# Half units of a logsumexp: three TensorE-biased heads, one exponential over two PSUM banks, GpSimd folding

## The chip, the cores and the metric

The kernel runs on 1 core of one Trainium2 chip. The metric is the time of one execution on the device, in microseconds (us). A run is called slow when it is over 1.5% above the fastest run of the same kernel in the same measurement, else fast. Ratios below use fast runs only.

Names: PE is TensorE, PEld its weight loads, ACT is ScalarE, DVE is VectorE, POOL is GpSimd. The clock that a profile shows is the share of PE's full clock that was granted. A warming matmul is one whose result nobody uses; it is there to keep PE busy. "The lock" is the prediction's name for something it assumed: that weighted sums of VectorE with two SBUF inputs and GpSimd's adds hold each other up. The trace of the kernel before had not shown it; the runs below measure it (such a sum 648 ns in "steady", and 416 with its factor in PSUM in "psum7"; GpSimd's third add 492 ns in "rows128" and 386 in "psum7"). A "half unit" is half of a tile of the input: 128 rows of 2048 numbers (1 MB).

## The reference

```python
B, S, D, H = 8, 2048, 2048, 8          # x: (B, S, D) float32, bias: (H, D // H)
x_heads = x.reshape(B, S, H, Dh).transpose(0, 2, 1, 3) + bias[None, :, None, :]
x_tiled = np.repeat(x_heads, 2, axis=2)
mx = x_tiled.max(axis=-1, keepdims=True)
lse = mx.squeeze(-1) + np.log(np.exp(x_tiled - mx).sum(axis=-1))
```

Each row of x holds 8 heads of 256 numbers. For each row and head the kernel needs the logarithm of the sum of exp(x + bias). The 134 MB of x are read once. The kernel subtracts no maximum, and is correct on this draw.

## The kernel before

There are 64 tiles of 2 x 128 rows (2 MB). A head's bias can enter in two ways. PE adds it: a bias matmul and an identity matmul accumulate x + bias in PSUM, and ACT takes the exponential from there. Or ACT takes exp(x), and VectorE multiplies by exp(bias) while it sums (a "weighted sum"). A few heads are added up by GpSimd: it halves the 256 elements by adding halves until 32 are left ("fold"), and VectorE reduces those. The closing stage (tiles 57 to 63) loads and works in half units:

```python
PROMPT_F1 = dict(pe=2, acc=2, g0=8, late=False, fold=1)   # 2 heads biased on PE and summed by ACT, 1 folded
PROMPT_F2 = dict(pe=2, acc=2, g0=8, late=False, fold=2)
SINGLE_F1 = dict(pe=1, acc=1, g0=8, late=False, fold=1)
TRIPLE = dict(pe=3, acc=3, g0=8, late=False, fold=0)
FOLD = 32
STAGES = [
    (0, (BULK,)),
    (54, (MIXED,)),
    (57, (PROMPT_F1, PROMPT_F1)),
    (62, (SINGLE_F1, SINGLE_F1)),
    (63, (PROMPT_F2, TRIPLE)),
]
# ... (cut)
    def put_bias(m, k0, k1):
        # ... (cut: bulk)
        for k in range(k0, k1, rows):
            for c in range(0, n, MM):                 # MM = 512
                # ... (cut)
                mm = nc.tensor.matmul(p, lhsT=ones3, rhs=each_row(b3, c, w, rows),
                                      start=True, stop=False)   # bf16, 3 rows: bias in three parts
    def keep_warm():
        for _ in range(NWARM):
            nc.tensor.matmul(tp[:, 0], lhsT=ident, rhs=ident, start=True, stop=True)

    def sum_biased(t, k, h, bank, p, mm, sums):       # one head: exp and sum by ACT
        act = nc.scalar.activation(out=xts[t % NBUF][:, k, h * Dh : (h + 1) * Dh], in_=p,
                                   func=ACT.Exp, accum_out=sums[:, k, h : h + 1])

    def weigh(t, v, h, dst, after):                   # one head: weighted sum by VectorE
        c = h * Dh
        if c < W0:
            w = one_ps[:, c - V0 : c - V0 + Dh]       # factors in PSUM
        elif c < W2:
            w = w_ps[:, c - W0 : c - W0 + Dh]         # factors in PSUM
        else:
            w = w_sb[:, c - W1 : c - W1 + Dh]         # head 7: factors in SBUF
        # ... (cut: tensor_tensor_reduce, multiply and add)

    def fold(t, k, h0, h1, sums, after):              # multiply by w_sb, then halve to FOLD
        # ... (cut)
```

In a half unit of tiles 57 to 61, before the change, ACT takes one exponential of six heads and two of one head with a sum; VectorE makes five weighted sums; GpSimd multiplies one head by its factors and folds it.

The softmax here doesn't subtract the row's maximum and nothing guards it: scores larger than these inputs give would overflow.

Of the kernel before, what the change touches and what calls it, by code (L numbers as in the profile page):

```python
# [11 lines left out]
ACT = mybir.ActivationFunctionType  # L12
ALU = mybir.AluOpType
# [7 lines left out]
NBUF = 8  # L21

NEARLY = 5

NWARM = 3



# [1 line left out]



BULK = dict(pe=3, acc=1, g0=4, late=True, fold=0)
MIXED = dict(pe=1, acc=1, g0=4, late=False, fold=0)
PROMPT_F1 = dict(pe=2, acc=2, g0=8, late=False, fold=1)
PROMPT_F2 = dict(pe=2, acc=2, g0=8, late=False, fold=2)
SINGLE_F1 = dict(pe=1, acc=1, g0=8, late=False, fold=1)
TRIPLE = dict(pe=3, acc=3, g0=8, late=False, fold=0)
FOLD = 32

STAGES = [
    (0, (BULK,)),
    (54, (MIXED,)),
    (57, (PROMPT_F1, PROMPT_F1)),
    (62, (SINGLE_F1, SINGLE_F1)),
    (63, (PROMPT_F2, TRIPLE)),
]

LAST_COLS = [
    [(0, 512), (1280, 2048), (512, 1280)],  # L50
    [(0, 512), (768, 1280), (1280, 1792), (512, 768), (1792, 2048)],
]

# [2 lines left out]
def kernel(  # L56
# [6 lines left out]
    nc = tc.nc  # L63
    P = nc.NUM_PARTITIONS
    B, S, D = x.shape
    H, Dh = bias.shape
# [4 lines left out]
    T = B * NBLK  # L71
    T_PROMPT = STAGES[1][0]
    T_FACTORS = T // 2
    CPE = BULK["pe"] * Dh
    MM = 512
# [11 lines left out]
    w_sb = sb.tile([P, D - W1], F32, name="w_sb")  # L87
# [153 lines left out]
    n_ps = [0]  # L241


    bank_users = [[], []]

    def on_bank(i, ins):
        for j, u in bank_users[i // 2]:
            if j != i and u.ins.engine != ins.ins.engine:
                tc.declare_no_dep(ins.ins, u.ins, reason="another bank")
        bank_users[i // 2].append((i, ins))  # L250
        return ins

    def put_bias(m, k0, k1):



        if m["late"]:
            pair = pairs[n_ps[0] % 2]
            n_ps[0] += 1
            got = [one_ps, pair[:, 0:MM], pair[:, MM : 2 * MM]]  # L260

            parts = [(ones3, b3)]
            if n_ps[0] <= NEARLY:
                parts = [(ones3[0:1], bparts[:, i]) for i in range(3)]
            for h, p in enumerate(got):
                for i, (lhsT, b) in enumerate(parts):
                    nc.tensor.matmul(  # L267
                        p,
                        lhsT=lhsT,
                        rhs=each_row(b, h * Dh, Dh, K),  # L270
                        start=i == 0,
                        stop=False,
                    )
            return got + [pair]
        n = m["pe"] * Dh
        rows = min(k1 - k0, max(MM // n, 1))
        got = []
        for k in range(k0, k1, rows):
            for c in range(0, n, MM):
                w = min(n - c, MM)  # L280
                bank = n_ps[0] % len(ps)
                p = ps[bank][:, 0 : rows * w]
                n_ps[0] += 1
                mm = nc.tensor.matmul(
                    p,
                    lhsT=ones3,
                    rhs=each_row(b3, c, w, rows),
                    start=True,
                    stop=False,
                )  # L290
                on_bank(bank, mm)
                got.append((k, k + rows, c, w, bank, p))
        return got

    def add_x(m, t, k0, c0, c1, got):


        heads = []
        for ka, kb, c, w, bank, p in got:
            if not c0 <= c < c1:  # L300
                continue
            mm = nc.tensor.matmul(  # L302
                p,
                lhsT=ident,
                rhs=xts[t % NBUF][:, ka:kb, c : c + w],
                start=False,
                stop=True,
            )
            on_bank(bank, on_x(t, mm, [loads[t, k0, c0]]))
            for i in range(0, (kb - ka) * w, Dh):  # L310
                k, cw = divmod(i, w)
                heads.append((ka + k, (c + cw) // Dh, bank, p[:, i : i + Dh], mm))
        return heads

    def keep_warm():
        for _ in range(NWARM):
# [109 lines left out]
        )  # L426
        last_uses[t].append(on_x(t, ttr, [after]))

    def fold(t, k, h0, h1, sums, after):


        v = xts[t % NBUF][:, k, h0 * Dh : h1 * Dh]
        done = nc.gpsimd.tensor_tensor(  # L433
            out=v, in0=v, in1=w_sb[:, h0 * Dh - W1 : h1 * Dh - W1], op=ALU.mult
        )
        on_x(t, done, [after])
        v = v.rearrange("p (h j) -> p h j", j=Dh)
        n = Dh
        while n > FOLD:
            n //= 2  # L440
            done = nc.gpsimd.tensor_tensor(  # L441
                out=v[:, :, 0:n], in0=v[:, :, 0:n], in1=v[:, :, n : 2 * n], op=ALU.add
            )
            on_x(t, done, [])

        def add_up():
            red = nc.vector.tensor_reduce(
                out=sums[:, k, h0:h1],
                in_=v[:, :, 0:FOLD],
                op=ALU.add,  # L450
                axis=mybir.AxisListType.X,
            )
            on_x(t, red, [done])

        return add_up
# [60 lines left out]
    def flush(later_work):  # L516
        for f in later_work:
            f()
        later_work.clear()

    for t in range(T):
# [4 lines left out]
        for k0, k1, c0, c1 in pieces(t):  # L526
# [5 lines left out]
            if m["late"]:  # L532
                pe_part = late_heads(m, t, bias_here, sums)
            else:
                heads = add_x(m, t, k0, c0, c1, bias_here)

                def pe_part(t=t, heads=heads, sums=sums):
                    for k, h, bank, p, mm in heads:
                        sum_biased(t, k, h, bank, p, mm, sums)

            if c0 == 0:
                if next_units and not m["late"]:
                    bias_there = put_bias(*next_units.pop(0))
                if t > T_PROMPT and m["g0"] == H:
                    keep_warm()
                if m["g0"] < H:
                    add = g_add(m, t, k0, k1)
                if t < T - 1 or k0 == 0:
                    flush(for_pool)
# [1 line left out]
                first_factors()  # L551
            h0 = max(c0 // Dh, m["pe"])
            h1 = min(c1 // Dh, m["g0"])
            hf = max(h0, min(h1, H - m["fold"]))
            if h0 < h1 and not m["late"]:
                done = exp_inplace(
                    t, xt[:, k0:k1, h0 * Dh : h1 * Dh], loads[t, k0, c0]
                )
                if hf < h1:
                    for_pool.append(fold(t, k0, hf, h1, sums, done))  # L560
            if c0 == 0:
                flush(for_pe)
            if not m["late"]:
                for k in range(k0, k1):
                    for h in range(h0, hf):
                        weigh(
                            t,
                            xt[:, k, h * Dh : (h + 1) * Dh],
                            h,
                            sums[:, k, h : h + 1],  # L570
                            done,
                        )
# [55 lines left out]
```

## Time and profile before

| | before |
|---|---|
| time, first measurement | 325.62 us median of 3 (325.56 to 325.81) |
| span of the profile | 323.1 us |
| time less span of the profiled run | 325.31 - 323.1 = 2.2 us |
| data read, rate | 134.23 MB, 419 GB/s |
| last row of the sums done on VectorE | 319.64 us |

In a page row of groups, the columns are: line, engine, operation, output and inputs with shapes, count, busy us and mean ns of one, then the idle time just before such instructions and what ended it. In a row of the timeline: start, length, instruction, and in brackets the idle time before it. Two such rows of VectorE in the kernel before, which the prediction did not show, matter for what follows:

```profile
305.38 0.19 DVE L447 TENSOR_REDUCE R_last<-xb 128x1 f32<-128x32 f32 x1 [0.15 <-POOL xb L441]
307.46 0.18 DVE L447 TENSOR_REDUCE R_last<-xb 128x1 f32<-128x32 f32 x1 [0.20 <-POOL xb L441]
```

Once per half unit, from 305 us, VectorE waits 0.15 to 0.20 us for a fold. It has worked off its backlog and has some slack, though not much: under a tenth of the 2.08 us that a half unit takes.

### The profile page before, as it was taken

Reading aid. Unit: us, or ns where it says so; the run is one execution under the profiler, and the core shown is the slowest. Engines: PE = TensorE matmul, PEld = TensorE weight load, DVE = VectorE, ACT = ScalarE, POOL = GpSimd, SP = SyncE. Lnnn points to the kernel's source line nnn. Section 1 sums busy time; section 2 is a strip of 40 time slices with the busy share of each in tenths; the row PEclk is TensorE's granted clock in tenths of the full one; section 3 lists DMA queues with packets and bytes.
Section 4 is the critical chain, followed back from the end, with each engine's and each line's share of the span. In section 5 each row is a group of like instructions: output and inputs, shape, how many; then the busy total and the mean of one; then the engine's idle time right before and its main releaser. Section 6 shows DMA issues by size and latency. Waiting matters only on the chain.

```text
span 323.1 us, 2398 instructions
## 1 busy us (share of the span) xinstructions
PE 270.3 (84%) x691; PEld 102.9 (32%) x691; DVE 283.9 (88%) x306; ACT 265.8 (82%) x426; POOL 287.7 (89%) x120
## 2 busy tenths in 40 slices
PE   5999999889978769977869886888997786599984
PEld 2333333333323223322323322333333232035442
DVE  1037779999999998999899899898999999999995
ACT  1148679889869976988888978889998998899995
POOL 6939998999999999999999999999999999858874
PEclk9979799979979996998997997997999999559998
DMA  8999999999999999999999999999999999999995
GB/s 311 457 402 454 450 400 439 450 402 446 438 414 446 432 418 443 430 422 447 422 426 441 422 434 442 404 426 430 432 422 431 430 428 425 416 422 421 419 401 170
DMA packets 8830, 135.42 MB, mean 419 GB/s; under 512 B 1041, under 2 KB 1425, under 8 KB 2417
## 3 DMA queue, kind: packets, MB, share of 16 engines
q1 hardware_dynamic: 8720, 135.27, 98.6%
q8 instruction: 5, 0.08, 0.1%
q14 instruction: 7, 0.06, 0.0%
q10 hardware_dynamic: 98, 0.01, 0.0%
HBM read 134.23 MB, written 1.05 MB: 419 GB/s over the span
## 4 chain that ended last, share of the span: by engine, by line
DMA 40%; POOL 18%; ACT 17%; PE 14%; DVE 9%; issue 0%; SPq 0%; DVEq 0%
DMA xb<-in_x_dram 40%; POOL xb L376 18%; ACT xb L382 11%; DVE R L401 6%; PE pair L326 5%; PE one_ps L326 3%; PE pair L267 3%; ACT xb L357 2%; PE one_ps L267 2%; DVE xb L417 2%; PE pair L219 1%; ACT xb L337 1%; DVE xb L394 1%; ACT res L471 1%; ACT xb L344 1%; DMA brow<-in_bias_dram 1%
## 5 line engine op out<-in xcount | busy, mean ns | idle before, releaser
L376 POOL TENSOR_TENSOR xb<-xb,b_rep 128x2048 f32<-128x2048 f32 x57 | 257.6, 4539 | 20.7 <-DMA xb<-in_x_dram 20.6
L401 DVE TENSOR_REDUCE R<-xb 128x14 f32<-128x3584 f32 (+1 forms) x56 | 214.5, 3830 | 1.9
L382 ACT ACTIVATE xb<-xb 128x2560 f32<-128x2560 f32 (+5 forms) x77 | 157.1, 2050 | 10.3 <-POOL xb L376 10.1
L326 PE MATMUL pair<-xb,ident 128*128 128x512 f32 x216 | 114.3, 656 | 0.0
L326 PE MATMUL one_ps<-xb,ident 128*128 128x512 f32 x108 | 67.5, 710 | 11.5 <-DMA xb<-in_x_dram 11.5
L344 ACT ACTIVATE xb<-pair 128x1024 f32<-128x1024 f32 x54 | 55.5, 1027 | 23.2 <-PE pair L326 23.0
L326 PEld LDWEIGHTS pair<-xb,ident 128*128 128x128 f32 x216 | 46.2, 214 | 61.3 <-issue 61.3
L394 DVE TENSOR_TENSOR xb<-xb,w_ps 128x512 f32<-128x512 f32 x54 | 36.7, 681 | 26.2 <-ACT xb L382 26.2
L337 ACT ACTIVATE xb<-one_ps 128x256 f32<-128x256 f32 x108 | 40.0, 380 | 6.6 <-PE one_ps L326 6.6
L267 PEld LDWEIGHTS <-ones 3*128 3x128 bf16 (+1 forms) x192 | 16.9, 95 | 80.8 <-issue 71.4
L267 PE MATMUL one_ps<-b,ones 3*128 3x512 bf16 x49 | 18.6, 380 | 25.4 <-ACT xb L337 25.3
L267 PE MATMUL pair<-b,ones 3*128 3x512 bf16 x98 | 29.0, 375 | 0.0
L326 PEld LDWEIGHTS one_ps<-xb,ident 128*128 128x128 f32 x108 | 17.2, 200 | 33.9 <-DMA xb<-in_x_dram 18.0
L302 PE MATMUL pair<-xb,ident 128*128 128x512 f32 (+1 forms) x36 | 21.7, 689 | 5.7 <-DMA xb<-in_x_dram 5.7
L417 DVE CUSTOM_DVE_ANT_0 xb<-xb,w_ps 128x256 f32<-128x256 f32 x61 | 22.4, 418 | 0.0
L337 ACT ACTIVATION_READ_ACCUMULATOR xb<-one_ps 128x1 f32 x108 | 22.3, 207 | 0.0
L441 POOL TENSOR_TENSOR xb<-xb 128x128 f32<-128x128 f32 (+3 forms) x39 | 13.8, 355 | 3.1
L433 POOL TENSOR_TENSOR xb<-xb,w_sb 128x256 f32<-128x256 f32 (+1 forms) x13 | 10.0, 771 | 5.2 <-ACT xb L382 4.5
L317 PE MATMUL tp<-ident 128*128 128x128 f32 x84 | 13.7, 302 | 0.0
L317 PEld LDWEIGHTS tp<-ident 128*128 128x128 f32 x84 | 11.1, 200 | 3.5 <-issue 3.0
L357 ACT ACTIVATE xb<-pair 128x256 f32<-128x256 f32 x33 | 11.9, 364 | 0.0
L417 DVE CUSTOM_DVE_ANT_0 xb<-xb,one_ps 128x256 f32<-128x256 f32 x27 | 10.6, 415 | 0.1
(42 smaller groups left out, 83.4 us busy)
## 6 DMA issues: line engine op xcount, KB each, us to landing
xb<-in_x_dram SPq DMA_DIRECT2D x20, 4096.0 KB, 21.5
xb<-in_x_dram SPq DMA_DIRECT2D x17, 2048.0 KB, 22.7
xb<-in_x_dram SPq DMA_DIRECT2D x12, 1024.0 KB, 22.7
xb<-in_x_dram SPq DMA_DIRECT2D x4, 256.0 KB, 13.2
out_dram<-res SPq DMA_DIRECT2D x1, 896.0 KB, 6.7
xb<-in_x_dram SPq DMA_DIRECT2D x2, 384.0 KB, 15.8
xb<-in_x_dram SPq DMA_DIRECT2D x2, 128.0 KB, 6.3
out_dram<-res_last SPq DMA_DIRECT2D x1, 128.0 KB, 1.7
```

The lines of the kernel that those rows point to most:

```text
L267: nc.tensor.matmul(p, lhsT=lhsT, rhs=each_row(b, h * Dh, Dh, K), start=i == 0, stop=False,)
L302: mm = nc.tensor.matmul(p, lhsT=ident, rhs=xts[t % NBUF][:, ka:kb, c : c + w], start=False, stop=True,)
L317: nc.tensor.matmul(tp[:, 0], lhsT=ident, rhs=ident, start=True, stop=True)
L326: mm = nc.tensor.matmul(p, lhsT=ident, rhs=xts[t % NBUF][:, :, h * Dh : (h + 1) * Dh], start=False, stop=True,)
L337: act = nc.scalar.activation(out=xts[t % NBUF][:, k, 0:Dh], in_=got[0][:, k * Dh : (k + 1) * Dh], func=ACT.Exp, accum_out=sums[:, k, 0:1],)
L344: act = nc.scalar.activation(out=xts[t % NBUF][:, :, Dh : m["pe"] * Dh].rearrange("p k (h j) -> p h k j", j=Dh), in_=got[-1].rearrange("p ...
L357: act = nc.scalar.activation(out=xts[t % NBUF][:, k, h * Dh : (h + 1) * Dh], in_=p, func=ACT.Exp, accum_out=sums[:, k, h : h + 1],)
L376: add = nc.gpsimd.tensor_tensor(out=v, in0=v, in1=each_row(b_rep, c - G0, D - c, k1 - k0), op=ALU.add)
L382: return on_x(t, nc.scalar.activation(out=v, in_=v, func=ACT.Exp), [after])
L394: mul = nc.vector.tensor_tensor(out=f, in0=f, in1=each_row(w_ps, m["pe"] * Dh - W0, n, k1 - k0), op=ALU.mult,)
L401: red = nc.vector.tensor_reduce(out=sums[:, k0:k1, h0:H], in_=v.rearrange("p k (h j) -> p k h j", j=Dh), op=ALU.add, axis=mybir.AxisListTy ...
L417: ttr = nc.vector.tensor_tensor_reduce(out=v, in0=v, in1=w, scale=1.0, scalar=0.0, op0=ALU.mult, op1=ALU.add, accum_out=dst,)
```

## The change

The intent: relieve ACT, which paces the closing stage. Three heads are biased on PE; ACT takes their exponential in one instruction over two PSUM banks, without sums; GpSimd folds all three, and has no multiply any more, because the bias is already in. One mode serves all half units from tile 57 on, but the last. The core of the diff:

```diff
-NWARM = 3
+NWARM = 8
-PROMPT_F1 = dict(pe=2, acc=2, g0=8, late=False, fold=1)
-PROMPT_F2 = dict(pe=2, acc=2, g0=8, late=False, fold=2)
-SINGLE_F1 = dict(pe=1, acc=1, g0=8, late=False, fold=1)
+FOLDED = dict(pe=3, acc=0, g0=8, late=False)
-    (57, (PROMPT_F1, PROMPT_F1)),
-    (62, (SINGLE_F1, SINGLE_F1)),
-    (63, (PROMPT_F2, TRIPLE)),
+    (57, (FOLDED, FOLDED)),
+    (63, (FOLDED, TRIPLE)),
@@
+    def exp_biased(t, k, n, heads):
+        _, _, bank, _, mm = heads[-1]
+        act = nc.scalar.activation(
+            out=xts[t % NBUF][:, k, 0 : n * Dh],
+            in_=pairs[bank // 2][:, 0 : n * Dh],
+            func=ACT.Exp,
+        )
+        on_bank(bank, on_x(t, act, [mm]), both=True)
+        return act
@@ fold
-        done = nc.gpsimd.tensor_tensor(
-            out=v, in0=v, in1=w_sb[:, h0 * Dh - W1 : h1 * Dh - W1], op=ALU.mult
-        )
+        v = xts[t % NBUF][:, k, 0 : n * Dh].rearrange("p (h j) -> p h j", j=Dh)
+        w = Dh
+        done = after
+        while w > FOLD:
+            w //= 2
+            add = nc.gpsimd.tensor_tensor(
+                out=v[:, :, 0:w], in0=v[:, :, 0:w], in1=v[:, :, w : 2 * w], op=ALU.add
+            )
+            done = on_x(t, add, [done])
@@ main loop
+                    if m["acc"] == 0:
+                        done = exp_biased(t, k, m["pe"], heads)
+                        for_pool.append(fold(t, k, m["pe"], sums, done))
+                        return
@@
-                if next_units and not m["late"]:
-                    bias_there = put_bias(*next_units.pop(0))
-                if t > T_PROMPT and m["g0"] == H:
+                if t > T_PROMPT and m["g0"] < H:
                     keep_warm()
@@
-            if c0 == 0:
+            if c0 == 0 or t == T - 1 and k0 == 0:
                 flush(for_pe)
+            if c0 == 0 and next_units and not m["late"]:
+                bias_there = put_bias(*next_units.pop(0))
 (cut: bank tracking, the last tile's columns, removal of the arguments h0, h1)
```

The warming matmuls move too: three per half unit before, none in the half units after; eight at each of tiles 55 and 56 instead.

More of the change, by code (lines that the diff above doesn't have):

```diff
@@ L23 @@
 NEARLY = 5
-NWARM = 3
-BULK = dict(pe=3, acc=1, g0=4, late=True, fold=0)
-MIXED = dict(pe=1, acc=1, g0=4, late=False, fold=0)
-PROMPT_F1 = dict(pe=2, acc=2, g0=8, late=False, fold=1)
-PROMPT_F2 = dict(pe=2, acc=2, g0=8, late=False, fold=2)
-SINGLE_F1 = dict(pe=1, acc=1, g0=8, late=False, fold=1)
-TRIPLE = dict(pe=3, acc=3, g0=8, late=False, fold=0)
+NWARM = 8
+BULK = dict(pe=3, acc=1, g0=4, late=True)
+MIXED = dict(pe=1, acc=1, g0=4, late=False)
+FOLDED = dict(pe=3, acc=0, g0=8, late=False)
+TRIPLE = dict(pe=3, acc=3, g0=8, late=False)
 FOLD = 32
@@ L43 @@
     (54, (MIXED,)),
-    (57, (PROMPT_F1, PROMPT_F1)),
-    (62, (SINGLE_F1, SINGLE_F1)),
-    (63, (PROMPT_F2, TRIPLE)),
+    (57, (FOLDED, FOLDED)),
+    (63, (FOLDED, TRIPLE)),
 ]
 LAST_COLS = [
-    [(0, 512), (1280, 2048), (512, 1280)],
+    [(0, 768), (1280, 2048), (768, 1280)],
     [(0, 512), (768, 1280), (1280, 1792), (512, 768), (1792, 2048)],
@@ L244, with on_bank @@
     bank_users = [[], []]
-    def on_bank(i, ins):
-        for j, u in bank_users[i // 2]:
-            if j != i and u.ins.engine != ins.ins.engine:
+    def on_bank(i, ins, both=False):
+        pair = i // 2
+        i = None if both else i
+        for j, u in bank_users[pair]:
+            if None not in (i, j) and j != i and u.ins.engine != ins.ins.engine:
                 tc.declare_no_dep(ins.ins, u.ins, reason="another bank")
-        bank_users[i // 2].append((i, ins))
+        bank_users[pair].append((i, ins))
         return ins
@@ L275, in put_bias @@
         n = m["pe"] * Dh
+        if n > MM:
+            n_ps[0] += n_ps[0] % 2
         rows = min(k1 - k0, max(MM // n, 1))
@@ L427, in weigh, with fold @@
         last_uses[t].append(on_x(t, ttr, [after]))
-    def fold(t, k, h0, h1, sums, after):
-        v = xts[t % NBUF][:, k, h0 * Dh : h1 * Dh]
-        done = nc.gpsimd.tensor_tensor(
-            out=v, in0=v, in1=w_sb[:, h0 * Dh - W1 : h1 * Dh - W1], op=ALU.mult
-        )
-        on_x(t, done, [after])
-        v = v.rearrange("p (h j) -> p h j", j=Dh)
-        n = Dh
-        while n > FOLD:
-            n //= 2
-            done = nc.gpsimd.tensor_tensor(
-                out=v[:, :, 0:n], in0=v[:, :, 0:n], in1=v[:, :, n : 2 * n], op=ALU.add
+    def fold(t, k, n, sums, after):
+        v = xts[t % NBUF][:, k, 0 : n * Dh].rearrange("p (h j) -> p h j", j=Dh)
[5 more added lines that the diff above has]
+                out=v[:, :, 0:w], in0=v[:, :, 0:w], in1=v[:, :, w : 2 * w], op=ALU.add
             )
-            on_x(t, done, [])
+            done = on_x(t, add, [done])
         def add_up():
             red = nc.vector.tensor_reduce(
-                out=sums[:, k, h0:h1],
+                out=sums[:, k, 0:n],
                 in_=v[:, :, 0:FOLD],
@@ L535, with pe_part @@
                 heads = add_x(m, t, k0, c0, c1, bias_here)
-                def pe_part(t=t, heads=heads, sums=sums):
+                def pe_part(t=t, m=m, k=k0, heads=heads, sums=sums):
+                    if m["acc"] == 0:
+                        done = exp_biased(t, k, m["pe"], heads)
+                        for_pool.append(fold(t, k, m["pe"], sums, done))
+                        return
                     for k, h, bank, p, mm in heads:
@@ L553 @@
             h1 = min(c1 // Dh, m["g0"])
-            hf = max(h0, min(h1, H - m["fold"]))
             if h0 < h1 and not m["late"]:
@@ L558 @@
                 )
-                if hf < h1:
-                    for_pool.append(fold(t, k0, hf, h1, sums, done))
-            if c0 == 0:
+            if c0 == 0 or t == T - 1 and k0 == 0:
                 flush(for_pe)
+            if c0 == 0 and next_units and not m["late"]:
+                bias_there = put_bias(*next_units.pop(0))
             if not m["late"]:
                 for k in range(k0, k1):
-                    for h in range(h0, hf):
+                    for h in range(h0, h1):
                         weigh(
```

## The prediction

> **What bounds the kernel now.** I read the page's 40 slices first, then a table by stage, then the chain that ended last, then the groups of the closing stage.
>
> The slices say that the kernel is a DMA stream with a closing stage behind it:
>
> ```profile
> PEclk9979799979979996998997997997999999559998
> DMA  8999999999999999999999999999999999999995
> ```
>
> The DMA engines are full from the second slice to the last but one, and 134 MB have to be read, so only the time after the last load can move by much. The change touches nothing before the stage in which tiles are loaded as half units (1 MB, about 2.5 us of stream each): tiles 57 to 63, from about 283 us. The reader sees also the two slices at half PE clock just before it.
>
> The stage table (stretch: its length, busy us of PE, PEld, DVE, ACT, POOL with counts, granted clock, DMA share, GB/s):
>
> ```profile
> 282.00:290.00 8.00, 7.43 (x14) 2.98 (x14) 8.00 (x25) 7.59 (x13) 4.70 (x2) 0.50 1.01 421
> 290.00:292.00 2.00, 2.00 (x10) 0.94 (x9) 2.00 (x5) 2.00 (x4) 1.31 (x3) 0.84 1.03 430
> 292.00:304.00 12.00, 12.00 (x54) 6.06 (x53) 12.00 (x70) 12.00 (x31) 9.84 (x23) 1.00 1.01 417
> 304.00:312.50 8.50, 7.17 (x34) 4.09 (x35) 7.72 (x45) 8.50 (x21) 6.97 (x17) 1.00 1.01 413
> ```
>
> From 292 to 304 ACT and DVE have no idle time while GpSimd has 18%: the stage starts late and works its backlog off at ACT's pace, 2.08 us per half unit (see below) against 2.5 us of arrival. By 312.5 the backlog is gone: PE waits for each load.
>
> The end, from the chain in order of time (start, length, what):
>
> ```profile
> 312.54 1.60 ACT xb L382
> 314.16 0.42 DVE xb L417
> ...
> 319.50 0.14 DVE R_last L447
> 319.64 0.14 issue
> 319.78 0.32 PE tp L482
> 320.11 0.38 ACT res_last L488
> ```
>
> ACT's exponential of half unit (62,1) at 312.54 follows its load; then DVE runs without a gap through its weighted sums to 319.6, and the transpose, logarithm and store take 3.5 us more, to the span's 323.1. The last load (issued 312.4, 5.2 us to landing) is there at 317.6. So 2 us at most could be gained here, and whatever makes an engine carry a backlog into 313 us costs its full length.
>
> [...]the weighing factors lie in PSUM (one_ps, w_ps) and their sums take 414 to 418 ns beside a busy GpSimd. [...]one sum in the whole program reads w_sb, from SBUF, at 319.07, when GpSimd's last instruction was within 0.1 us of its end.
> [...]
> [...]
> [...]
>
> **The change part by part**, per half unit. The groups of GpSimd and ACT from 287 to 320 us (busy us, mean ns):
>
> ```profile
> L433 POOL TENSOR_TENSOR xb<-xb,w_sb 128x256 f32<-128x256 f32 x12 | 8.8, 729 | 5.2 <-ACT xb L382 4.5
> L441 POOL TENSOR_TENSOR xb<-xb 128x128 f32<-128x128 f32 x13 | 5.9, 457 | 1.0
> L441 POOL TENSOR_TENSOR xb<-xb 128x64 f32<-128x64 f32 x13 | 4.2, 320 | 1.0
> L433 POOL TENSOR_TENSOR xb<-xb,w_sb 128x512 f32<-128x512 f32 x1 | 1.3, 1274 | 0.0
> L441 POOL TENSOR_TENSOR xb<-xb 128x256 f32<-128x256 f32 x1 | 0.7, 730 | 0.1
> L382 ACT ACTIVATE xb<-xb 128x1536 f32<-128x1536 f32 x10 | 14.6, 1467 | 0.0
> L357 ACT ACTIVATE xb<-pair 128x256 f32<-128x256 f32 x27 | 9.6, 357 | 0.0
> ```
>
> ACT before: the 1536-wide exponential and two summing ones of 256, 1.37 + 0.71 = 2.08 us by the chain's steps. After: one of 1280 (1467 less 213 ns, the difference of the 1792 and 1536 forms, is 1254; less 0.10 of overlap, 1.15) and one of 768 (826 as an SBUF form, 0.73): 1.88 us. **ACT gains 0.20.**
>
> DVE before: five weighted sums at 0.34 and a reduce of 32. After: again five (heads 3 to 7) and a reduce of 96 (0.25 by the step of 33 ns from 32 to 64). No gain; but head 7's factor is w_sb, in SBUF, so now every half unit has a two-SBUF-input sum beside GpSimd's adds.
>
> GpSimd before: 0.73 multiply, 1.19 for three adds, 0.08 us gaps: about 2.08. After: adds of 384, 192 and 96 elements. Midway between measured widths: (730+1274)/2 = 1002, (457+730)/2 = 594, (320+457)/2 = 389 ns; sum 1.98, with three gaps of 0.08, **2.22 us. GpSimd becomes the slowest engine of the stage.** The addition of heads, 1 to 3, outweighs the multiply saved.
>
> PE: 768 columns per half unit, not 512, so 1.5 times the float32 work: 0.9 to 1.3 us plus about 0.3 for bias, at full clock. This fits 1.88. At half clock, about 3.2, it doesn't fit 2.5. The eight warming matmuls at each of tiles 55 and 56 make PE busy from 282.6 without a break, so I expect full clock by 289 or 290, as before.
>
> Order matters twice. First, a half unit's biased exponential now comes after the next one's plain exponential, and its fold after that. Second, the bias of a unit needs both banks of a pair, so that of (58,0) waits for the biased exponential of (57,0); and on PE it stands ahead of the four transposes that the logarithm of batch 6 waits for. ACT waits there.
>
> Sum, from the trace's 287.17, where ACT starts tile 56's last exponential (released by GpSimd, unchanged): +1.81 = 288.98; two of 1280, 291.29; biased (57,0), 292.0; then bias 0.33, transposes 0.60, handovers 0.1, so the logarithm at 293.05 instead of 292.0; +0.92, 293.97; plain (58,0), 295.1; biased (57,1), 295.85. GpSimd folds (57,0) from 292.1 to 294.3, and (57,1) can start at 295.9. From there 12 folds, (57,1) to (63,0), at 2.22: 322.5. ACT, faster, releases each in time, having caught up with the loads near (61,0). The closing reduces wait for the last fold: +0.25, 322.8; +3.5, **326.3 us of span, 3.2 more than now.** Without the lock: 325.6 + 3.2 = 328.8.
>
> The lock: each w_sb sum can hold GpSimd for 0.34 us, of which the 0.08 gap hides some: up to 0.27 per fold, 12 folds, 3.2 us. Full: 332.0. I take it as about 70% likely and usually not whole, and put **330.8**.
>
> **The rivals.** (a) ACT's gain decides: the backlog is gone 2 us sooner, and DVE, which has one sum less in each half of tile 62 and one more in tile 63, ends sooner: 324 to 325. For it: ACT has no idle time from 292 to 312.5. Against: it needs the 13 folds done between 292.1 and DVE's present end at 319.4, 2.10 each with no wait at the logarithm, and the widths say 2.22. (b) The lock binds fully and DVE and GpSimd take turns: fold 1.0 + 0.59 + sum 0.35 + 0.39 and gaps, 2.5 us, the rate of the loads, so the backlog is never worked off: 332 to 333. [...]Against: nothing in this trace has shown a blocked sum. (c) PE falls to half clock in the stage, where no warming is left: 3.2 us per unit until warm again, 1 to 5 us more. For it: the clock fell in the bulk stage at a PE load that is about as high.[...] (d) The stream is hidden anyway: loads are all issued by buffers freed 8 tiles earlier, none by these folds, so the last landing stays at 317.6.
>
> **Range and chances.** No lock and no other trouble gives 328.8; half the lock 330.4; all of it 332.0, turn-taking 333. I estimate interpolated fold widths good to 0.08 us, 1 us over 12. So 327.4 to 333.3. Slower by over 2% means above 332.1: a good part of (b) and (c), 0.26. Faster by over 2% is below 319, under the end of the loads: 0.02. Within 2%: 0.72.
>
> **What will show it.** GpSimd's adds of 384, 192, 96 at 1.00, 0.59, 0.39 us and 13 folds nearly back to back from 296 us; ACT waiting about 1 us before the logarithm at 293; the chain's end running through GpSimd's adds and a reduce, no longer DVE's sums; w_sb sums or the adds after them longer by up to 1.0 or 0.3 us if the lock is real; the clock at 1.0 from 290 on; the last load at 317.6. The prediction is wrong if the folds take 2.0 or less, if DVE doesn't wait for them, or if the clock stays at half.

## The result, and the profile after

| kernel | runs | median us | lowest to highest | ratio of fast runs to before |
|---|---|---|---|---|
| before, same chip | | 325.59 | 325.28 to 325.81 | 1 |
| after | 4 timed | 335.39 | 328.65 to 340.52 | 1.0121 (1.0074 to 1.0167) |

A ratio is the mean time of one kernel's fast runs over that of the other's fast runs of the same rounds, so it is not quite the ratio of the medians quoted here. The four timed runs were 340.45, 328.65, 340.52 and 330.34 us; a fifth run took 333.58. The kernel before never left 325.06 to 326.19 in all its measurements. So the change made the kernel 1.2% slower in its fast runs, which is within 2%, and gave it runs that are up to 4.6% slower (340.52 against 325.59).

The first profile fell on a slow run (340.45 us, span 338.4). Its slices of clock and stream:

```profile
PEclk9997799979978997998999698999998969965555
DMA  8999999999999999999999999999999999999700
```

The stream ends as before: the last slice with loads, the 38th of 40, spans 313 to 321 us, and the last load is issued at 312.3 us and lands at 317.6 (before: 312.4 and 317.6). What is new are the four last slices at half PE clock. The chain in order of time (start, length, what) shows what they do:

```profile
292.15 0.48 PE pair L286 x2
...
296.13 0.48 PE pair L286 x2
296.61 1.50 PE pair L304 x4
298.10 0.75 PE pair L286 x2
298.85 2.86 PE pair L304 x4
```

L286 is the bias (3 active rows), L304 the identity matmul that adds x. At 298 us each step grows by half or to twice its length, and from there to the end the chain is PE alone: 0.75 + 2.86 = 3.61 us per half unit, against 2.5 us of arrival. The clock is 0.50 from 298.0 us and never comes back, although PE is busy for 34.00 of the 34.00 us from 298 to 332.

The same kernel was run again with more rounds (the experiment "again" below), and that profile is of a fast run (329.86 us, span 327.8). The stage table, in the stretches that the prediction shows for before (length, then busy us of PE, PEld, DVE, ACT, POOL, clock, DMA share, GB/s):

```profile
282.00:290.00 8.00, 8.00 (x37) 4.72 (x35) 8.00 (x27) 6.79 (x8) 4.77 (x2) 0.94 1.02 425
290.00:292.00 2.00, 0.09 (x1) 0.09 (x1) 2.00 (x10) 2.00 (x3) 0.00 (x0) 1.00 0.98 401
292.00:304.00 12.00, 11.32 (x30) 4.44 (x29) 12.00 (x55) 10.10 (x12) 9.20 (x14) 0.72 1.02 421
304.00:312.50 8.50, 8.50 (x28) 3.63 (x27) 8.50 (x45) 8.37 (x10) 7.95 (x12) 1.00 1.01 413
```

ACT is relieved: it has idle time from 292 to 304, where it had none. PE is idle from 290 to 292 (2.11 us in its timeline), because the next bias matmuls wait for the biased exponential to free both banks; the clock then falls here too, at 293.2 us (mean of the stretch 0.72), but is back at 300.0. VectorE, alone of the five, has no idle time in any stretch. The groups of GpSimd and VectorE from 294 to 324 us:

```profile
L450 POOL TENSOR_TENSOR xb<-xb 128x384 f32<-128x384 f32 x12 | 12.2, 1014 | 1.9 <-ACT xb L320 1.8
L450 POOL TENSOR_TENSOR xb<-xb 128x192 f32<-128x192 f32 x12 | 7.2, 596 | 0.9
L450 POOL TENSOR_TENSOR xb<-xb 128x96 f32<-128x96 f32 x13 | 5.7, 439 | 1.0
```

```profile
L430 DVE CUSTOM_DVE_ANT_0 xb<-xb,w_ps 128x256 f32<-128x256 f32 x56 | 20.0, 410 | 0.0
L430 DVE CUSTOM_DVE_ANT_0 xb<-xb,w_sb 128x256 f32<-128x256 f32 x14 | 9.2, 655 | 0.0
L456 DVE TENSOR_REDUCE R_last<-xb 128x3 f32<-128x96 f32 x13 | 3.1, 243 | 0.0
```

The first two adds are as predicted; the third takes 439 ns in place of 0.39 us. GpSimd's idle time is small, 3.8 us in the 30. But VectorE's idle column is 0.0 throughout, and its sums with two SBUF inputs (w_sb) take 655 ns where those with a factor in PSUM take 410. The end of the chain:

```profile
319.35 0.63 DVE xb L430
...
323.87 0.34 DVE R_last L456 x2
324.20 0.14 issue
```

It runs through VectorE's sums, not through GpSimd's adds: the last of 13 folds ends at 322.37, VectorE 1.8 us later. The step of 0.63 us is the w_sb sum; the others are 0.33.

### The profile page after: what moved, and what is told of

It reads as the page before. It is cut to its first block, busy times and chain, and to the rows that moved or that the text cites. A ratio compares the mean times of both kernels' runs of the same rounds, so it can differ in the third digit from the quotient of the medians.

```text
span 338.4 us, 2322 instructions
## 1 busy us (share of the span) xinstructions
PE 287.3 (85%) x678; PEld 107.4 (32%) x678; DVE 289.4 (86%) x304; ACT 264.0 (78%) x391; POOL 290.3 (86%) x107
## 4 chain that ended last, share of the span: by engine, by line
DMA 32%; PE 28%; DVE 24%; ACT 12%; POOL 3%; issue 1%; SPq 0%; DVEq 0%
DMA xb<-in_x_dram 32%; DVE R L414 20%; PE pair L304 8%; ACT xb L395 8%; PE pair L339 6%; PE one_ps L339 4%; DVE xb L407 3%; PE pair L267 3%; POOL xb L389 3%; PE pair L286 2%; PE one_ps L267 2%; ACT res L480 1%; PE pair L216 1%; ACT xb L357 1%; ACT xb L350 1%; PE tp L470 1%
## 5 line engine op out<-in xcount | busy, mean ns | idle before, releaser
L395 ACT ACTIVATE xb<-xb 128x2560 f32<-128x2560 f32 (+5 forms) x77 | 154.0, 2008 | 9.5 <-POOL xb L389 9.3
L339 PE MATMUL pair<-xb,ident 128*128 128x512 f32 x216 | 116.3, 666 | 0.0
L339 PEld LDWEIGHTS pair<-xb,ident 128*128 128x128 f32 x216 | 46.7, 216 | 62.7 <-issue 62.7
L450 POOL TENSOR_TENSOR xb<-xb 128x384 f32<-128x384 f32 (+2 forms) x39 | 26.4, 680 | 20.1 <-ACT xb L320 18.0
L304 PE MATMUL pair<-xb,ident 128*128 128x512 f32 (+1 forms) x62 | 39.7, 782 | 1.8 <-DMA xb<-in_x_dram 1.8
L304 PEld LDWEIGHTS pair<-xb,ident 128*128 128x128 f32 x62 | 15.6, 280 | 24.3 <-issue 18.5
L320 ACT ACTIVATE xb<-pair 128x768 f32<-128x768 f32 x13 | 10.4, 803 | 15.5 <-PE pair L304 15.5
L286 PE MATMUL pair<-b,ones 3*128 3x512 bf16 (+1 forms) x31 | 11.5, 456 | 5.7 <-ACT xb L320 4.5
L480 ACT ACTIVATE res<-tp 32x1024 f32<-32x1024 f32 x7 | 7.1, 1013 | 5.6 <-PE tp L470 5.6
L430 DVE CUSTOM_DVE_ANT_0 xb<-xb,w_sb 128x256 f32<-128x256 f32 x14 | 10.5, 749 | 0.0
```

What stands on the lines that cost most here:

```text
L304: mm = nc.tensor.matmul(p, lhsT=ident, rhs=xts[t % NBUF][:, ka:kb, c : c + w], start=False, stop=True,)
L339: mm = nc.tensor.matmul(p, lhsT=ident, rhs=xts[t % NBUF][:, :, h * Dh : (h + 1) * Dh], start=False, stop=True,)
L395: return on_x(t, nc.scalar.activation(out=v, in_=v, func=ACT.Exp), [after])
L430: ttr = nc.vector.tensor_tensor_reduce(out=v, in0=v, in1=w, scale=1.0, scalar=0.0, op0=ALU.mult, op1=ALU.add, accum_out=dst,)
L450: add = nc.gpsimd.tensor_tensor(out=v[:, :, 0:w], in0=v[:, :, 0:w], in1=v[:, :, w : 2 * w], op=ALU.add)
```

## The experiments

Twelve kernels were run. "Before" was timed in each call on the same chip. The unaltered changed kernel has 17 runs in all (5 above, 6 in each of two repeats); 7 of them lie above 331.5 us.

| label | what | median us | lowest to highest | ratio to before (95%) |
|---|---|---|---|---|
| again | unaltered | 330.76 | 329.86 to 335.14 | 1.0173 (1.0141 to 1.0205) |
| again2 | unaltered | 329.18 | 328.67 to 336.36 | 1.0130 (1.0096 to 1.0165) |
| warm2 | 2 warming matmuls per half unit | 329.20 | 328.86 to 329.82 | 1.0118 (1.0103 to 1.0132) |
| cold3 | no warming at all | 329.09 | 328.49 to 329.46 | 1.0111 (1.0095 to 1.0126) |
| cold128 | no warming, bias with 128 rows | 329.63 | 328.57 to 330.71 | 1.0118 (1.0091 to 1.0145) |
| rows128 | bias with 128 rows | 329.06 | 328.61 to 329.45 | 1.0108 (1.0094 to 1.0121) |
| steady | 128 rows, 1 warming matmul per half unit | 328.98 | 328.71 to 330.12 | 1.0112 (1.0099 to 1.0126) |
| psum7 | steady, head 7's factor in PSUM | 328.08 | 327.72 to 328.30 | 1.0078 (1.0065 to 1.0091) |
| lnfirst | steady, transposes before the bias | 328.15 | 327.75 to 329.82 | 1.0094 (1.0073 to 1.0115) |
| fold64 | steady, GpSimd folds to 64 | 328.13 | 327.98 to 330.05 | 1.0099 (1.0077 to 1.0122) |
| best | psum7, lnfirst and fold64 together, more warming at tile 57 | 326.44 | 326.18 to 328.36 | 1.0047 (1.0024 to 1.0070) |
| bestalt | best, folds to 64 and 32 in turn | 326.36 | 326.13 to 327.80 | 1.0036 (1.0017 to 1.0054) |

At a threshold of 2% all of these are the same as before, except "again", whose interval straddles it. There are two questions. Why do some runs take 333 to 340 us? And why are even the fast ones 3 to 5 us slower than before?

### The slow runs: the unaltered kernel, and a warmed one

"again" is the changed kernel as it is.

> The changed kernel unmodified. Theory A (TensorE's clock): its runs fall into two groups, one near 328.6 to 330.4 us where the clock stays at full through the closing stage, one of 333 to 341 us where it falls to half there and stays; the granted clock over the whole run orders the runs (about 0.91 for the quick, 0.87 to 0.89 for the slow). Theory B (the lock between VectorE and GpSimd, or anything that is there in every run): the times spread around one value and the clock doesn't order them.

It gave 329.86, 330.31, 330.80, 333.60, 330.72 and 335.14 us. These are not the two groups that theory A expected, and the clock orders them only in part: the slowest run has the lowest mean clock (0.882), but 333.60 us came with 0.904 and 330.80 with 0.899. "warm2" adds two full-size warming matmuls per half unit:

```diff
-                if t > T_PROMPT and m["g0"] < H:
-                    keep_warm()
+                if t > T_PROMPT:
+                    keep_warm(NWARM if m["g0"] < H else 2)
```

> Two warming 128x128 matmuls after each half unit's bias and data matmuls, as the kernel before had three. Theory A: no run above 332 us, granted clock 1.0 from 290 us to the end in the profile, times 328 to 331 us, that is still about 3 us slower than the kernel before, because GpSimd's folds (2.2 us each, 12 of them from 296 us) are what is left. Theory B: slow runs of 335 to 340 us still occur. If the prediction's lock cost is fully there, the folds take 2.5 us each and the time is near 332.

Four runs, 328.86 to 329.82, none slow; in its profile the clock is 1.0 from 280.6 to 325.0 us. With warming the slow runs are gone, in these four, but the time stays 1.2% above before. So the clock goes with the slow runs (one of them was profiled: 0.50 from 298.0 us) and has little to do with the rest. This doesn't say yet why PE, busy without a break in that run, stayed at half clock.

### Why the clock doesn't come back: 3 rows or 128

Two kernels without any warming matmul differ in one thing: whether the bias matmuls have 3 active rows or 128. Theory C is a conjecture that the 3 rows keep PE at half clock; rival D sees no difference between the two. "cold3":

```diff
-NWARM = 8
+NWARM = 0
```

> No warming matmuls at all, bias matmuls with 3 active rows as they are. TensorE enters the closing stage at half clock. Theory C[...]: half clock to the end of the stage, 3.6 us per half unit, 12 or 13 of them from about 287 us: 338 to 343 us in every run. Rival D ([...]the stuck clock of the profiled run was an accident): full clock by 296 us and 329 to 333 us.

"cold128" does the same, and pads the bias operands to 128 rows, of which 125 are zero. The columns, the data type and the result are the same:

```diff
-NWARM = 8
+NWARM = 0
-    ones3 = sb.tile([3, P], BF16, name="ones3")
-    b3 = sb.tile([3, CPE], BF16, name="b3")
+    ones_all = sb.tile([P, P], BF16, name="ones_all")
+    b_all = sb.tile([P, CPE], BF16, name="b_all")
+    ones3, b3 = ones_all[0:3], b_all[0:3]
+    nc.vector.memset(ones_all, 0.0)
+    nc.vector.memset(b_all, 0.0)
@@ put_bias, half units
-                    lhsT=ones3,
-                    rhs=each_row(b3, c, w, rows),
+                    lhsT=ones_all,
+                    rhs=each_row(b_all, c, w, rows),
```

> As cold3, with no warming matmul, but the bias matmuls of the MIXED and half-unit stages have 128 active rows, those after the third zero: the same number of matmuls, columns and cycles. Theory C: the stage starts at half clock and is at full clock after one to three windows (by about 297 us), 329 to 334 us. Rival D or any theory in which only the gaps count: the same time as cold3.

The expected time of "cold3" was wrong: 329.09 us, not 338 to 343. By the times alone rival D did better: it forecast 329 to 333 us and full clock by 296 us for "cold3" (329.09, clock back at 296.16) and no difference to "cold128" (329.63). So half clock up to 296 us cost no time that shows, and the times say nothing for 3 rows against 128. The traces say more about the clock itself. In the traces of "before" and "after" its changes lie whole multiples of 3.413 us apart, so I cut the stage into windows of that length. "cold3", where PE works at half clock from 282 us on (same columns as above):

```profile
282.50:285.92 3.42, 3.42 (x5) 1.03 (x6) 3.42 (x10) 3.42 (x6) 3.42 (x1) 0.50 1.01 422
285.92:289.33 3.41, 3.41 (x7) 1.30 (x6) 3.41 (x10) 2.45 (x4) 1.05 (x1) 0.50 1.00 418
...
292.74:296.16 3.42, 3.42 (x9) 1.61 (x8) 3.42 (x20) 2.38 (x3) 1.23 (x3) 0.50 1.01 422
296.16:299.57 3.41, 3.01 (x11) 1.29 (x11) 2.47 (x15) 3.41 (x5) 2.70 (x4) 1.00 1.02 423
```

and "cold128":

```profile
282.93:286.35 3.42, 3.42 (x6) 1.19 (x6) 3.42 (x10) 3.20 (x6) 3.42 (x1) 0.50 1.01 422
286.35:289.76 3.41, 2.67 (x9) 1.16 (x8) 3.41 (x13) 2.68 (x2) 0.70 (x1) 1.00 1.00 418
```

In both the first window is filled by PE (3.42 of 3.42 us) with the same mixture: bias takes 0.82 us in it in "cold3" and 0.85 in "cold128". With 128 rows the next window runs at full clock (1.00); with 3 rows it stays at half (0.50). "cold3" came back, at 296.16, only after the window from 292.74, in which the four transposes stood and, by the records, almost no bias. Two filled windows of "cold3" were thus followed by half clock, where the one of "cold128" was followed by full clock. Rival D sees no such difference. The pair points to the rows of the bias; how they would act on the clock it doesn't show.

I then took all half-clock windows of the traces "before" and "after" (15 to 318 us) and worked out from the matmul records which share of each was covered by matmuls with 128 active rows. Of 36 windows, 27 had PE busy throughout (share of all matmuls 1.00). The 19 of these with 0.86 or more in full rows were all followed by full clock. Of the other eight, one with 0.79 (171.2 us in "before") was followed by full clock, one with 0.85 (283.8 us in "before") and six with 0.80 by half; the six are the stuck loop of the slow run. So this share alone doesn't decide what follows, and since some matmul records can be missing in a trace, the shares are rough. By the chain's steps the loop's own share is 2.86 of 3.61 us, 0.79. Why a loop that has fallen to half clock gets free in some runs and stays in others, no run shows.

### The slow runs once more: 128 rows alone

"rows128" is the changed kernel with only the padded bias, and its eight warming matmuls at tiles 55 and 56. "again2" is the unaltered kernel beside it.

```diff
 NWARM = 8
+    ones_all = sb.tile([P, P], BF16, name="ones_all")
+    b_all = sb.tile([P, CPE], BF16, name="b_all")
 (and the rest of the padded bias, as in cold128)
```

> The changed kernel with one thing altered: the bias matmuls have 128 active rows, 125 of them zeros[...] (no warming matmul added, eight at tiles 55 and 56 as in the change). Theory: the runs of 333 to 340 us of the changed kernel (4 of 11 so far) are those in which the clock falls at the gaps near 292 and 296 us[...]. Then a fall is followed by a return within one or two clock windows, no run is above 331.5, and the median is 328.5 to 330.7. Rival: slow runs come from elsewhere (the bulk stage, the chip's state); then slow runs of 333 to 340 remain here as in the unaltered kernel beside it.

> The changed kernel unaltered, on the same chip as the run with 128-row bias. Theory: medians of 330 to 336, with at least one run of six above 332; ratio of fast runs 1.012 to 1.018. If none is above 331.5, this comparison decides nothing about the slow runs.

"rows128": 328.61 to 329.45, five runs, none slow. Its profile doesn't test the expected return, because the clock never falls in it between 280.8 and 321.7 us; but in "cold128", "psum7" and "lnfirst" it falls between 291 and 294 us, and is back after one window each time (means of 0.79, 0.84 and 0.79 from 292 to 300 us, 1.00 from 300 to 316). "again2": 328.67, 332.57, 329.23, 328.98, 336.36 and 329.13, two of six above 331.5, as expected, though the median, 329.18, missed the expected 330 to 336. Over all kernels with 128-row bias (cold128, rows128 and the six below, which have a few warming matmuls besides) there are 43 runs, the highest at 330.71; of the unaltered kernel 7 of 17 lie above 331.5. But 34 of the 43 have warming matmuls too, and by "warm2" these may suffice alone. For the rows alone it is 0 of 9 ("cold128", "rows128") against 7 of 17, which chance would give about once in 30. So the rows are the likely cause, not a certain one. The rival, that slow runs come from the bulk stage or the chip, finds no support. One thing doesn't fit neatly: "cold3" had 3 rows, no warming and no slow run, in four. Too few to say that it has none.

### The fast runs: three suspects on one base

"steady" is the base for the next three: 128-row bias and one warming matmul per half unit, so the clock is out of the comparison as far as possible (in its profile it is 1.00 from 284 to 316 us).

```diff
 (the padded bias as in cold128)
+                    keep_warm(NWARM if m["g0"] < H else 1)
```

> The changed kernel with bias matmuls of 128 active rows (125 of them zeros) and one warming matmul per half unit. Theory: the slow and scattered times of the changed kernel come only from the TensorE clock[...]. Then the clock stays at 1.0 from about 286 us to the end, no run is slower than 330.5, and the folds alone set the end: 12 folds of 2.16 to 2.23 us from 296.1, time 328.2 to 329.5 (ratio 1.008 to 1.013). PE should need 0.42 + 1.49 + 0.22 = 2.13 us per half unit, no longer the 2.36 it needed with two warming matmuls. Rival: PE paces the stage even when warm; then the time falls by half of that difference or more below the kernel with two warming matmuls (329.2), toward 326.5 to 328.

328.98 us, as the theory of the folds said, but its profile says something else: VectorE has no wait of 0.1 us or more after 222 us, the chain in the whole closing stage, to 322.9 us, is VectorE alone, and GpSimd's last fold ends at 322.16. The time was right for a reason that was at least half wrong. From 294 to 324 us:

```profile
L453 POOL TENSOR_TENSOR xb<-xb 128x192 f32<-128x192 f32 x12 | 7.8, 649 | 0.9
L433 DVE CUSTOM_DVE_ANT_0 xb<-xb,w_sb 128x256 f32<-128x256 f32 x14 | 9.1, 648 | 0.0
```

Both engines are held up here, VectorE in its w_sb sums (648 ns, against 416 for the same sums in "psum7" below) and GpSimd a little in its second add (649 ns against 592). GpSimd's folds follow each other without a wait too, with the same step of 2.16 us as VectorE's half units, so the chain by way of VectorE is only the later of two that run in step.

**Head 7's factor in PSUM** ("psum7"). From tile 58 on one_ps[:, 0:256] is free, so exp(bias) of head 7 goes there, and no sum has two SBUF inputs any more:

```diff
+    T_SPARE = STAGES[2][0] + 1
+    def last_factor():
+        c = W2 - G0
+        nc.scalar.activation(
+            out=one_ps[:, 0:Dh], in_=b_rep[:, c : c + Dh], func=ACT.Exp
+        )
@@ weigh
-        if c < W0:
+        if c == W2 and t >= T_SPARE:
+            w = one_ps[:, 0:Dh]
+        elif c < W0:
```

> As 'steady', but from tile 58 on head 7's factor is read from PSUM, so that no weighted sum of VectorE has two SBUF inputs beside GpSimd's adds. If the lock between VectorE and GpSimd costs time on the path: w_sb sums (425 to 749 ns so far) become 414 to 418 ns, the third add falls from up to 490 to 388 ns, a fold from up to 2.23 to 2.15 us, and the time is 0.3 to 1.0 us below 'steady'. If the lock lies off the path (VectorE waits, but has slack): same time within 0.2 us, though the w_sb rows become short.

328.08 us, 0.90 less than "steady", clear of noise (the intervals of the two ratios don't overlap), and all five runs within 0.6 us. The groups from 294 to 324 us:

```profile
L463 POOL TENSOR_TENSOR xb<-xb 128x192 f32<-128x192 f32 x12 | 7.1, 592 | 0.9
L463 POOL TENSOR_TENSOR xb<-xb 128x96 f32<-128x96 f32 x13 | 5.0, 386 | 1.0
L443 DVE CUSTOM_DVE_ANT_0 xb<-xb,one_ps 128x256 f32<-128x256 f32 x12 | 5.0, 416 | 0.0
L469 DVE TENSOR_REDUCE R_last<-xb 128x3 f32<-128x96 f32 x13 | 3.3, 254 | 1.8 <-POOL xb L463 0.5
```

The sums of head 7 take 416 ns in place of 648 in "steady", and VectorE waits again (0.14 us per half unit). The chain runs through GpSimd's adds, with a step of 2.10 us per half unit. So the w_sb sums beside GpSimd's adds did cost time, 232 ns each on VectorE in "steady", and it was on the path. Who pays differs from run to run. In "rows128" it is GpSimd:

```profile
L453 POOL TENSOR_TENSOR xb<-xb 128x96 f32<-128x96 f32 x13 | 6.4, 492 | 1.0
L433 DVE CUSTOM_DVE_ANT_0 xb<-xb,w_sb 128x256 f32<-128x256 f32 x14 | 6.3, 450 | 0.0
```

There the third add takes 492 ns in place of 386, a fold 2.23 us, and the chain runs through the folds, as the prediction had it. In "again", "again2" and "steady" VectorE pays most (about 0.70 us for most w_sb sums, in place of 0.42; GpSimd loses another 0.06 in one of its adds), and a half unit takes it 2.16 us. Most half units of a run show the same pattern. The times don't show who pays: 329.06 us in "rows128", 328.98 in "steady". There is a regularity in the eight profiles of fast runs that fold to 32 with w_sb in use. Take the start of VectorE's first 2.28 us reduce of the stage before (tile 54) as its entry: VectorE paid most of it where the entry was at 282.50 us or later (lnfirst 282.50, again2 282.78, steady 282.83, again 284.02, cold128 284.05), GpSimd where it was earlier (cold3 282.09, warm2 282.16, rows128 282.25). I have not tested this by moving the entry.

**Transposes before the bias** ("lnfirst"). The wait before the logarithm of batch 6 goes:

```diff
+            if c0 == 0 and k0 == K - 1 and m["acc"] == 0:
+                finish_due(t)                       # the four transposes and the logarithm
             if c0 == 0 and next_units and not m["late"]:
                 bias_there = put_bias(*next_units.pop(0))
```

> As 'steady', but the four transposes of batch 6 stand ahead of the bias of (58,0) on PE. If the wait before the logarithm delays the fold chain, as predicted: ACT's wait falls from 1.1 us to under 0.2, fold (57,1) starts 0.8 to 1.1 us earlier (near 295.2), and the time is 0.8 to 1.1 us below 'steady'. If the end is paced by something other than the folds (PE, VectorE, the loads): under 0.3 us.

ACT's wait, in the view of waits of "steady":

```profile
ACT res L483 <- PE tp L473: 1.0, 1, 1.0
```

In "lnfirst" the same view has no wait over this stretch; ACT's logarithm follows at once, and the next biased exponentials come 1.4 us earlier than in the timeline of "steady" (293.85 and 295.70 here, 295.23 and 297.08 there):

```profile
291.79 1.00 ACT L483 ACTIVATE res<-tp 32x1024 f32<-32x1024 f32 x1
...
293.85 0.78 ACT L323 ACTIVATE xb<-pair 128x768 f32<-128x768 f32 x1
```

The folds end at 320.76, 1.4 us before those of "steady". The median is 0.83 us lower, as expected, but the interval of its ratio overlaps that of "steady", two of six runs lie at 329.6 to 329.8, and the trace doesn't bear the gain out: VectorE still sets the end, and from its entry to its end it took 40.08 us here and 40.07 in "steady" (37.67 in the kernel before, waits included).

**Folding to 64** ("fold64"). GpSimd makes two adds, VectorE reduces 192 elements:

```diff
-FOLD = 32
+FOLD = 64
```

> As 'steady', but GpSimd folds to 64 elements (two adds, 1.00 + 0.60 + gaps = 1.70 us per half unit in place of 2.18) and VectorE reduces 192 per half unit in place of 96 (about 0.1 us more). If the folds set the end: 12 x 0.48 = 5.8 us come off the fold chain, another engine takes over (VectorE at about 2.05 to 2.2 us per half unit, PE at 2.13, or the loads), and the time is 1.0 to 2.5 us below 'steady', 326.0 to 328.0. If another engine sets it already: within 0.4 us of 'steady'.

The median is 0.85 us lower, between the two expectations (1.0 to 2.5, or within 0.4) and so a miss of both. Two of six runs lie at 330.05, the intervals overlap here too, and again VectorE took the same: 40.10 us. GpSimd was done at 319.67 and waited; VectorE's w_sb sums were shorter (558 ns in place of 648) and reduced more (343 ns in place of 243). In the profiles the 0.75 us between the ends are all in the entry: 282.05 here, 282.83 in "steady". So in these two profiles the folds were not what set the end. The edits of "fold64" and "lnfirst" change nothing before tile 57, so they can hardly be what moved the entry. Why it was earlier here than in "steady" stays open.

That VectorE's end can follow its entry also shows in the fast runs of the unaltered kernel: "again" entered at 284.02 and took 329.86 us, "again2" entered at 282.78 and took 328.67: 1.24 and 1.19 us apart. In these runs VectorE carries a backlog from the bulk stage and never works it off, so what delays it there (entries from 282.05 to 284.05 us) comes out at the end. In "psum7", where it has slack, the five runs are within 0.6 us.

### All together

"best" has the padded bias, one warming matmul per half unit (six in those of tile 57), the transposes first, head 7's factor in PSUM, and folds to 64.

```diff
 (the edits of steady, psum7, lnfirst and fold64)
-                    keep_warm(NWARM if m["g0"] < H else 1)
+                    keep_warm(NWARM if m["g0"] < H else 6 if t == STAGES[2][0] else 1)
```

> All cures together: 128-row bias, one warming matmul per half unit (six at tile 57), transposes ahead of the bias, head 7's factor in PSUM, GpSimd folds to 64. If GpSimd, VectorE and their lock are the three near-equal limits found so far, no single one of them remains: GpSimd 1.70 us and VectorE 1.97 us per half unit, VectorE still carrying its backlog from the bulk stage. From the run that folds to 64: VectorE's end at 322.15 less 14 locks of about 0.14 us on average (558 less 418 ns), so near 320.2, against 319.6 in the kernel before: time 325.8 to 326.8, ratio 1.001 to 1.004. If a gain remains hidden by something else: above 327.3.

326.44 us, in the expected range, and 2.5 us below "steady"; two of six runs lie at 328.3, outside it. GpSimd now waits, VectorE doesn't:

```profile
L463 POOL TENSOR_TENSOR xb<-xb 128x384 f32<-128x384 f32 x12 | 12.0, 1003 | 5.4 <-ACT xb L331 5.4
L469 DVE TENSOR_REDUCE R_last<-xb 128x3 f32<-128x192 f32 x13 | 4.4, 346 | 0.0
```

VectorE took 38.36 us from its entry at 282.17. The sum of the three single gains in the medians is 0.90 + 0.83 + 0.85 = 2.6 us, but as shown two of the three did not shorten VectorE's path alone. That they pay once head 7's factor is in PSUM is the likely reading; no run adds them one by one to "psum7".

"bestalt" lets the first half of a tile fold to 64 and the second to 32, so that VectorE reduces less:

```diff
-        while w > FOLD:
+        end = 2 * FOLD if k == 0 else FOLD
+        while w > end:
-                in_=v[:, :, 0:FOLD],
+                in_=v[:, :, 0:end],
```

> As 'best', but GpSimd folds to 64 only for the first half of a tile and to 32 for the second. In 'best' VectorE had no idle time and GpSimd 0.17 to 0.8 us per half unit. If VectorE's work alone sets the end of 'best': a reduce of 96 in place of 192 saves 0.09 us in 6 of 13 half units, 0.5 us in all: 325.7 to 326.2, against 326.44, still not below the kernel before (325.5). If GpSimd comes back onto the path: 326.4 to 327.3.

326.36 us: the same as "best" within their scatter, so this expectation missed, by 0.2 us. Its profile is of a run of 327.49 us, not of the median. In it VectorE's two sums with w_sb that are left, in tile 57, took 1048 ns each (those in "best" 567), which eats more than the 0.5 us, and VectorE entered at 282.94 us (282.17 in "best"). Inconclusive on the size of the reduce.

No kernel of mine beats the one before. "bestalt" is 0.36% above it.

## Why the prediction was right or wrong

The time on record was 330.8 us, 327.4 to 333.3, most likely within 2%. The fast runs are within 2% (1.0121) and their medians in the three measurements lie in the range; the median that counted the slow runs, 335.39, does not. Step by step:

- **The stream and its end.** Right. The last load lands at 317.6 us before and after.
- **ACT gains.** Right: 1.16 + 0.70 = 1.86 us per half unit by the chain's steps, predicted 1.88.
- **The wait before the logarithm.** Right: predicted "about 1 us", measured 1.11 in the fast profile and 1.0 in "steady". "lnfirst" took it away and the folds ended 1.4 us earlier.
- **The adds.** Predicted 1.00, 0.59 and 0.39; measured 1.02, 0.59 and 0.39 where no sum beside them reads w_sb ("psum7").
- **"2.22 us. GpSimd becomes the slowest engine of the stage."** The term was mis-sized. With no w_sb sum beside it a fold step is 2.10 us ("psum7"): the sum counted a gap of 0.08 three times, but there are two, and the next fold's first add starts about 0.03 us before the last one's end. Over 12 folds that is 1.4 us too much.
- **The lock.** Predicted up to 0.27 us per fold, 3.2 us in all, and paid by GpSimd: an estimate from the 0.34 us of a sum and the gap of 0.08, put at about 70%. An effect was measured, but on GpSimd it cost 2.23 less 2.10, 0.13 us per fold ("rows128"), half of the most that was allowed. In sum a fold came to 2.23 where 2.22 was predicted without a lock and 2.49 with a full one. Two errors cancelled, which is luck.
- **"DVE ... No gain".** The step that failed for many fast runs (five of the eight profiles above, among them both of the unaltered kernel; in "rows128", "warm2" and "cold3" VectorE did wait for the folds). The count of VectorE's work was right, five sums and a reduce. But the prediction let the lock fall on GpSimd alone, and so left VectorE at 5 x 0.34 + 0.25 = 1.95 us, although it allowed for longer w_sb sums in its list of what to look for. In "again", "again2" and "steady" VectorE pays about 0.3 us in most half units and needs 2.16, as long as the folds, and it brings a backlog along. The end was then set by VectorE's sums, not "running through GpSimd's adds and a reduce".
- **Half clock in the stage.** The prediction gave it too little weight; 6 of the 17 runs lie above 333.3. Its own stage table was a warning: from 282 to 290 us PE is busy for 7.43 of 8.00 us at a clock of 0.50. The gap near 292 us was in the working (the bias waits for both banks), but not the fall of the clock after it (at 293.2 us in the profile of "again", and at 298.0 in the slow run), and in the slow run PE then stayed busy at half clock to the end. "cold3" against "cold128" points to the 3-row bias, 0.75 of the loop's 3.61 us, without settling it.
- **Its own signs of being wrong.** Two of three were seen: VectorE did not wait for the folds ("again", "again2", "steady"), and the clock stayed at half (the slow run). Only the folds stayed above 2.0 us.
- **The rivals.** (a), ACT's gain decides: not seen, in no run. (b), turn-taking of 2.5 us per fold: not seen; 2.16 to 2.23. (c), half clock: seen in the slow runs, with more than the 1 to 5 us given to it (340.5 against fast runs of 328.7 to 330.3). (d): right.

So for the fast runs the verdict, the slower fold and the lock held, and one of two carriers of the end was missed; the risk that made the spread, half clock, was put at 1 to 5 us where the slow runs lost up to 12.

What stays open: whether "lnfirst" and "fold64" gain anything by themselves, since their medians fell, but not clear of noise, and VectorE's path did not get shorter; what sets VectorE's entry; and whether that entry decides who pays the lock.

## What to carry to other kernels

When an engine is relieved, look at which of the others has the least slack over the whole stage, and at every pair of them that may hold each other up: here the fold and the weighted sums were both at the limit, and the w_sb sums beside the adds cost time on either of them (0.13 us per fold in "rows128", about 0.3 us per half unit of VectorE in "steady"). Look at the clock too where PE comes out of a gap: in the slow run PE was busy for 34.00 of 34.00 us at a clock of 0.50, with 3-row bias matmuls in the loop; with the bias padded to 128 rows 0 of 9 runs lie above 331.5, without 7 of 17. Ask of a median that fits whether the trace says the same: two expectations here ("steady" and "lnfirst") were met by the time and not by the trace.
